# Second feed-forward products by a seven-product scheme on 2x2 blocks, on one Trainium2 core

## The chip, the core and the metric

One core of a Trainium2 chip runs the whole kernel as one program. The metric is the device time of one execution in microseconds; lower is better. A core has TensorE (PE, matmuls; its weight loads are shown apart as PEld), VectorE (DVE), ScalarE (ACT), GpSimd (POOL), SyncE (SP, which here issues DMAs), an on-chip memory SBUF and the accumulator memory PSUM, of which the kernel uses eight banks of 128 x 512 float32.

## The reference

Two blocks of a small transformer trunk over 512 tokens of width 1024, all in float32: a first block with windowed attention, a gated convolution and a mixture of experts, then two layers that each have a mixer and a feed-forward stage. The change touches only these two feed-forward stages:

```python
def sqrelu_mlp(u, w1, w2):
    return jnp.square(jax.nn.relu(u @ w1)) @ w2
...
for layer in range(DEPTH_2):
    ...
    h = h + sqrelu_mlp(rms_norm(h, mlp_norm[layer]), mlp_w1[layer], mlp_w2[layer])
return rms_norm(h, final_norm)
```

`u` is 512 x 1024, `w1` is 1024 x 4096, `w2` is 4096 x 1024.

## The kernel before

**Products.** Every float32 operand is split into a high part (rounded to the type that TensorE takes, `F32R`) and a low part (the rest). A product of two such operands is three matmuls, high by high, high by low and low by high (`mm3`, lines 184 to 188). One matmul has a stationary block of 128 x 128 and a moving block of 128 x 512, and adds into one PSUM bank.

**The feed-forward stage** (`mlp`, from line 1380) goes through the 4096 inner features in four chunks `c` of 1024. In a chunk, the first products (`fm`) make inner slices of 128 features x 512 tokens: four weight units `m{l}u{c}{u}` of 1024 x 256, two slices each, eight slices, 24 matmuls per slice. A slice goes from its bank through `evac`: relu on ScalarE (line 1391), square on VectorE (1392), high part on ScalarE (1393), low part on VectorE (1394), into `hTh` and `hTl`, four tiles of 8 KB per partition in all. Then the second products: for each half `n` of the 1024 output columns and each half `u` of the chunk's features one weight unit `m{l}d{c}{n}/{u}` of 512 x 512. `tm` keeps four banks, one for each 128 tokens, over both units, and `add_x` (line 374, VectorE) adds each full bank to the residual `x`. In the last half of the last chunk `tm_rows` goes row block by row block, so that `step` can normalise one block of 128 tokens (for the next mixer, or for the output) while the next is computed.

**Weights.** `Weights.units` is the list of all weight blocks in the order of use (`plan`, `plan_mlp`). `dma` loads one as raw float32 from SyncE's queue (line 72); `split` makes its high part on ScalarE (line 92) and its low part on VectorE (line 93), in two halves of 128 x 1024 each. `take` gives a unit to the products; `done` gives its two tiles back and calls `ahead`, which splits up to two units ahead (`cuts`) and loads up to four ahead (`look`) as far as there is room.

**Room.** All large tiles lie in 19 slots (`NQ`) of 8 KB per partition: a raw block takes one, a split unit two, `x` two, the split input `xT` of the stage four (`self.xq`, given back at the last chunk). `q` takes the slot that has been free for the longest, and whoever writes it waits until its last user is done. `reserve` (set by `need`) keeps slots back from the weights for tiles that come soon.

**Order.** The kernel is written as one stream of operations; the framework orders each engine's instructions by their dependencies, earlier ones first among those that it takes to be ready, and sets the semaphores. Engines then run their own lists strictly in order.

Of the kernel before, what the change touches and what calls it, by code (L numbers as in the profile page):

```python
# [12 lines left out]
F32 = mybir.dt.float32  # L13
F32R = mybir.dt.float32r
BF = mybir.dt.bfloat16
I32 = mybir.dt.int32
AF = mybir.ActivationFunctionType
OP = mybir.AluOpType
AX = mybir.AxisListType

T = 512
# [27 lines left out]
class Weights:  # L49
# [14 lines left out]
    def add(self, key, shape, parts, whole=False):  # L64
        self.units.append((key, shape, parts, whole))

    def dma(self):
        i = self.n_dma
        key, shape, parts, _ = self.units[i]
        r = self.k.q(shape, F32, "wr")  # L70
        for sl, src in parts:
            self.k.nc.sync.dma_start(r[sl], src)
        self.raw[i] = r
        self.n_dma += 1

    def split(self):
        i = self.n_cut
        if i == self.n_dma:
            self.dma()
        k, nc = self.k, self.k.nc  # L80
        key, shape, parts, whole = self.units[i]
        r = self.raw.pop(i)
        self.n_cut += 1
        if whole:
            self.cut[i] = (r,)
            return
        h = k.q(shape, F32R, "wh")
        lo = k.q(shape, F32R, "wl")
        a, n = shape[-2] // 2, (slice(None),) * (len(shape) - 2)
        for s, eng in zip((slice(0, a), slice(a, shape[-2])), self.engines or (nc.vector, nc.vector)):  # L90
            s = (*n, s)
            nc.scalar.copy(h[s], r[s])  # L92
            eng.tensor_tensor(lo[s], r[s], h[s].bitcast(F32), op=OP.subtract)  # L93
        k.put(r)
        self.cut[i] = (h, lo)

    def ahead(self):
        cut, dma = self.cuts, self.look
        n, r, f = self.limit or len(self.units), self.reserve, self.k.freeq
        def ready():  # L100
            return sum(not u[3] for u in self.units[self.n_take:self.n_cut])
        while self.n_cut < n and ready() < cut and len(f) >= r + 2 + (self.n_cut == self.n_dma):
            self.split()
        r += 2 * max(0, cut - ready())
        while self.n_dma < min(self.n_take + dma, n) and len(f) >= r + 1:
            self.dma()
# [15 lines left out]
class Kern:  # L122
# [67 lines left out]
    def tm(self, key, xT, nk, n, evac, pump=0):  # L190

        for full in self.tm_gen(key, xT, nk, n, evac):
            if full:
                self.pump(pump)
# [477 lines left out]
def kt(w, p=128):  # L672
    return w.rearrange("(k p) f -> p k f", p=p)
# [7 lines left out]
class Trunk(Kern):  # L681
    def plan(self):
# [64 lines left out]
            tm(f"co{n}", I["c_w_out_2"][0], n * 512, 512)  # L747
        self.plan_mlp(1, fm, tm)

    def plan_mlp(self, l, fm, tm):  # L750
        w1, w2 = self.I["mlp_w1_2"][l], self.I["mlp_w2_2"][l]
        for c in range(4):
            for u in range(4):
                fm(f"m{l}u{c}{u}", w1, c * 1024 + u * 256, 256)
            for n in range(2):
                tm(f"m{l}d{c}{n}", w2[c * 1024:(c + 1) * 1024], n * 512, 512)


    def consts(self):
# [619 lines left out]

    def mlp(self, l, xT):  # L1380
        nc, wk = self.nc, self.wk
        for c in range(4):
            hs = [self.q([128, 4, T], F32R, "hTh") for _ in range(2)]
            ls = [self.q([128, 4, T], F32R, "hTl") for _ in range(2)]
            for us in ((0, 1), (2,), (3,)) if c == 0 else ((0,), (1,), (2,), (3,)):
                def evac(f, b):
                    g = us[0] * 2 + f
                    r = wk.tile([128, T], F32, name="relu", tag="a2", bufs=8)
                    s = wk.tile([128, T], F32, name="cv", tag="a2", bufs=8)
                    h, lo = hs[g // 4][:, g % 4], ls[g // 4][:, g % 4]  # L1390
                    nc.scalar.activation(r, b, AF.Relu)
                    nc.vector.tensor_mul(s, r, r)
                    nc.scalar.copy(h, s)
                    nc.vector.tensor_tensor(lo, s, h.bitcast(F32), op=OP.subtract)
                self.fm([f"m{l}u{c}{u}" for u in us], xT, 2, evac)
            if c == 3:
                self.put(*self.xq)
                self.need(4)
            hT = [(hs[k // 4][:, k % 4], ls[k // 4][:, k % 4]) for k in range(8)]
            for n in range(2):  # L1400
                if c < 3 or n == 0:
                    self.tm(f"m{l}d{c}{n}", hT, 4, 512, self.add_x(n))
                    continue
                if l == 0:
                    yT, step = self.norm_T(self.gain(self.I["attn_norm_2"][1]))
                else:
                    yT, step = None, self.final()
                self.tm_rows(f"m{l}d{c}{n}", hT, 512, self.add_x(n), step)
            self.put(*hs, *ls)
        return yT  # L1410

    def topk(self, sc):
# [594 lines left out]
```

## Time and profile before

| | |
|---|---|
| median of 3 runs | 2027.82 us (2024.48 to 2027.97) |
| profiled execution | 2025.49 us |
| its span | 2023.4 us |
| feed-forward stages in the span | about 1000 to 1350 us and 1647 to 2013 us |
| TensorE busy | 1917.4 us (95%) |
| VectorE busy | 1246.3 us (62%) |
| ScalarE busy | 900.1 us (44%) |
| GpSimd busy | 328.4 us (16%) |
| moved by DMA | 260.45 MB, 129 GB/s on average |

The span is the time from the first to the last instruction that the hardware profiler recorded; the execution's time has some 2 us around it. An engine's share is an average over very different stages; what a change in one stage is worth is read from that stage alone.

### The profile page before, as it was taken

What the parts mean: (1) busy time and instruction counts of PE and PEld (TensorE: products, weight loads), DVE (VectorE), ACT (ScalarE), POOL (GpSimd) and SP (SyncE); (2) the same over time, 40 slices, a digit from 0 to 9 for tenths busy, and PEclk for the clock granted to TensorE, in tenths of its full rate; (3) what the DMA queues carried; (4) which work ended last, traced back from release to release, by engine and by line L of the source; (5) the groups of instructions that cost most, each with busy time, mean ns of one, the idle gap of its engine ahead of it and who ended that gap; (6) DMA issues with size and microseconds to landing.
All of it is one profiled execution on the core that took longest, in us unless ns stands there. A gap on an engine that the chain in (4) does not pass through costs nothing.

```text
span 2023.4 us, 25745 instructions
## 1 busy us (share of the span) xinstructions
PE 1917.4 (95%) x9419; PEld 1510.2 (75%) x9419; DVE 1246.3 (62%) x2606; ACT 900.1 (44%) x1697; POOL 328.4 (16%) x436
## 2 busy tenths in 40 slices
PE   7999999699988699999999999999999999999997
PEld 6877887455544587687888888888878888888886
DVE  6865255697667679997544343456789954443343
ACT  4256222586666435547232232422589933232240
POOL 3022000143232001104200000020247620000001
PEclk9999999699999899999999999999999999999999
DMA  7111357699999411104232322342000133323221
GB/s 223 42 43 64 103 191 277 213 354 344 356 368 373 129 42 64 51 32 146 74 122 87 104 94 85 113 136 67 22 22 1 64 120 120 99 88 104 84 84 42
DMA packets 129156, 260.45 MB, mean 129 GB/s; under 512 B 9015, under 2 KB 63631, under 8 KB 129026
## 3 DMA queue, kind: packets, MB, share of 16 engines
q1 hardware_dynamic: 119554, 229.59, 32.4%
q0 software_dynamic: 5952, 16.52, 3.4%
q10 hardware_dynamic: 3520, 12.65, 1.6%
q8 instruction: 76, 1.25, 0.3%
q14 instruction: 54, 0.44, 0.1%
HBM read 245.89 MB, written 14.88 MB: 129 GB/s over the span
## 4 chain that ended last, share of the span: by engine, by line
PE 71%; DVE 11%; DMA 9%; ACT 4%; issue 3%; POOL 1%; SPq 0%; ACTq 0%; DVEq 0%; POOLq 0%
PE ps L188 18%; PE ps L186 18%; PE ps L187 18%; DMA wr<-in_w_up_e_dram 3%; PE ps L580 3%; DVE wl L93 3%; DMA wr<-in_w_gate_e_dram 2%; PE ps L539 2%; PE ps L1249 2%; DMA xd<-y,sidx 1%; ACT wh L92 1%; PE ps L479 1%; PE ps L481 1%; PE ps L292 1%; ACT P L505 1%
## 5 line engine op out<-in xcount | busy, mean ns | idle before, releaser
L93 DVE TENSOR_TENSOR wl<-wr,wh 128x1024 fp32r<-128x1024 f32 (+3 forms) x366 | 439.8, 1224 | 341.4 <-ACT wh L92 322.3
L92 ACT CAST wh<-wr 128x1024 fp32r<-128x1024 f32 (+3 forms) x366 | 368.5, 1036 | 516.2 <-PE ps L188 161.2
L186 PE MATMUL ps<-xTh,wh 128*128 128x512 f32 (+1 forms) x864 | 324.6, 376 | 0.3 <-ACT P L505 0.3
L188 PE MATMUL ps<-xTh,wl 128*128 128x512 f32 (+1 forms) x864 | 323.0, 374 | 0.3 <-DVE wl L93 0.3
L187 PE MATMUL ps<-xTl,wh 128*128 128x512 f32 (+1 forms) x864 | 323.2, 374 | 0.0
L186 PE MATMUL ps<-wh,hTh 128*128 128x512 f32 x512 | 199.4, 389 | 0.0
L188 PE MATMUL ps<-wh,hTl 128*128 128x512 f32 x512 | 199.2, 389 | 0.0
L187 PE MATMUL ps<-wl,hTh 128*128 128x512 f32 x512 | 199.2, 389 | 0.0
L188 PEld LDWEIGHTS ps<-xTh,wl 128*128 128x128 f32 x864 | 162.7, 188 | 29.3 <-DVE wl L93 0.8
L186 PEld LDWEIGHTS ps<-xTh,wh 128*128 128x128 f32 x864 | 162.8, 188 | 28.9 <-ACT P L505 0.6
L187 PEld LDWEIGHTS ps<-xTl,wh 128*128 128x128 f32 x864 | 162.9, 189 | 28.2 <-issue 0.2
L300 POOL TENSOR_TENSOR xn<-x,gB 128x1024 f32<-128x1024 f32 x16 | 38.4, 2401 | 734.4 <-DVE x L374 734.4
L374 DVE TENSOR_TENSOR x<-ps,x 128x512 f32<-128x512 f32 x88 | 60.7, 690 | 127.1 <-PE ps L188 127.1
L505 ACT ACTIVATE P<-ps,sm 128x512 f32<-128x512 f32 (+1 forms) x224 | 118.3, 532 | 16.1 <-DVE sm L493 12.9
L1200 PE MATMUL ps<-wl,xgT 128*112 128x512 f32 x256 | 111.2, 434 | 13.9 <-DVE wl L93 13.4
L186 PE MATMUL ps<-wh,xTh 128*128 128x512 f32 (+3 forms) x320 | 120.5, 377 | 0.9 <-DVE ik L435 0.9
L1249 PE MATMUL ps<-wr,hT 128*72 128x512 f32 x256 | 117.4, 594 | 4.0 <-ACT hT L1238 4.0
L188 PE MATMUL ps<-wh,xTl 128*128 128x512 f32 (+3 forms) x320 | 117.5, 368 | 0.7 <-DVE xTl L352 0.7
L187 PE MATMUL ps<-wl,xTh 128*128 128x512 f32 (+3 forms) x320 | 117.0, 367 | 0.0
L1199 PE MATMUL ps<-wh,xgT 128*112 128x512 f32 x256 | 109.5, 428 | 3.0 <-ACT wh L92 2.8
L187 PEld LDWEIGHTS ps<-wl,hTh 128*128 128x128 f32 x512 | 96.1, 188 | 20.0
L188 PEld LDWEIGHTS ps<-wh,hTl 128*128 128x128 f32 x512 | 96.1, 188 | 19.9
(452 smaller groups left out, 3510.9 us busy)
## 6 DMA issues: line engine op xcount, KB each, us to landing
wr<-in_mlp_w_dram SPq DMA_DIRECT2D x64, 1024.0 KB
wr<-in_w_gate_e_dram SPq DMA_DIRECT2D x64, 512.0 KB
wr<-in_w_up_e_dram SPq DMA_DIRECT2D x64, 512.0 KB
wr<-in_w_down_e_dram SPq DMA_DIRECT2D x32, 1024.0 KB
wr<-in_w_in_dram SPq DMA_DIRECT2D x17, 1024.0 KB
wr<-in_ab_w_in_dram SPq DMA_DIRECT2D x10, 1024.0 KB
wr<-in_c_w_in_dram SPq DMA_DIRECT2D x6, 1024.0 KB
wr<-in_w_out_dram SPq DMA_DIRECT2D x4, 1024.0 KB
```

The source lines that it names most:

```text
L92: nc.scalar.copy(h[s], r[s])
L93: eng.tensor_tensor(lo[s], r[s], h[s].bitcast(F32), op=OP.subtract)
L186: mm(ps, ah, bh, start=first, stop=False)
L187: mm(ps, ah, bl, start=False, stop=False)
L188: mm(ps, al, bh, start=False, stop=last)
L374: self.nc.vector.tensor_tensor(xs, b, xs, op=OP.add)
L505: nc.scalar.activation(P[s][:, p:p + c.stop - c.start], b[:, c], AF.Exp, bias=m[:, 0, t:t + 1], accum_out=m[:, 1, t:t + 1])
L539: nc.tensor.transpose(b[:, c:c + 128], P[s][:, p:p + 128], self.idf)
L580: nc.tensor.matmul(o, v, x[:, cs], start=start, stop=a.closes and g == 2 and z == len(vx) - 1, skip_group_check=True)
L1199: nc.tensor.matmul(b[0:M], x, h, start=first, stop=False)
L1200: nc.tensor.matmul(b[0:M], x, lo, start=False, stop=last)
L1249: nc.tensor.matmul(b[0:HM], hq[:, k], w[0][:, k, s], start=k == 0, stop=k == 1)
```

## The change

The chunk's second product, tokens x features by features x columns, is seen as a product of 2 x 2 blocks: the 512 tokens are two halves of 256, the chunk's 1024 features are the even and the odd slices, the 1024 output columns are two halves of 512. Instead of the eight block products it makes seven (Strassen's method in its form with shared sums), of sums of weight blocks and sums of activation blocks, both made in float32 on VectorE before the split into high and low parts:

- **Weight blocks.** `add7` puts seven units per chunk on the list in place of four. Four of them load a block (b11, b12, b22, b21, of 512 x 512, every other group of 128 features); four units form a difference in place first (`sums`), and raw blocks stay until the last unit that needs them (`free`). A unit that loads nothing is passed over by `dma`.
- **Activations.** `evac` works on pairs of slices. Of the even one it splits the first 256 tokens (`A11`, in work tiles) and forms one difference of 256 columns; of the odd one it splits all (`B2`), forms one sum of 256, splits it with the difference (`S31`), forms two more differences of 256, and splits these (`S24`). Six tiles of 8 KB hold what four held.
- **Products.** Each of the seven is 2 x 12 matmuls (two blocks of 128 tokens, 4 slices, 3 matmuls) of the same shapes as before. Products share banks: after each product `add_x` adds the bank as it stands to one quarter of `x`, and a later product adds on in the same bank (`home`). The order is 11, T1, T2, 22, T3, 21, T4, in the last chunk 11, T1, T2, 22, 21, T3, T4, there with `step` for the first two row blocks after 21 and for the last two after their parts of T4. In the first layer's last chunk the four slots of the next stage's input are taken before the second products, not in their middle.

```diff
--- before.py
+++ after.py
@@ -64,12 +64,30 @@
     def add(self, key, shape, parts, whole=False):
         self.units.append((key, shape, parts, whole))
 
+    def add7(self, key, shape, parts, order):
+
+        b11, b12, b21, b22 = parts
+        rec = {"11": (b11, 0, [], 0, ()), "T1": (b12, 1, [(0, 1, 0)], 0, ()), "T2": (b22, 2, [(0, 2, 0)], 0, ()),
+               "22": (None, 0, [(1, 2, 1)], 2, (2,)), "T3": (None, 0, [], 1, (1,)),
+               "21": (b21, 3, [(0, 3, 0)], 3, (3,)), "T4": (None, 0, [], 0, (0,))}
+        group = {}
+        for o in order:
+            load, place, sums, src, free = rec[o]
+            self.units.append((f"{key}/{o}", shape, load, (group, place, sums, src, free)))
+
     def dma(self):
         i = self.n_dma
-        key, shape, parts, _ = self.units[i]
+        key, shape, parts, how = self.units[i]
+        if parts is None:
+            self.n_dma += 1
+            return
         r = self.k.q(shape, F32, "wr")
         for sl, src in parts:
             self.k.nc.sync.dma_start(r[sl], src)
+        if isinstance(how, tuple):
+            how[0][how[1]] = r
         self.raw[i] = r
         self.n_dma += 1
 
@@ -79,26 +97,33 @@
             self.dma()
         k, nc = self.k, self.k.nc
         key, shape, parts, whole = self.units[i]
-        r = self.raw.pop(i)
+        r = self.raw.pop(i, None)
         self.n_cut += 1
-        if whole:
+        if whole is True:
             self.cut[i] = (r,)
             return
+        sums, frees = (), (r,)
+        if whole:
+            g, _, sums, src, frees = whole
+            sums = [[g[x] for x in y] for y in sums]
+            r, frees = g[src], [g[x] for x in frees]
         h = k.q(shape, F32R, "wh")
         lo = k.q(shape, F32R, "wl")
         a, n = shape[-2] // 2, (slice(None),) * (len(shape) - 2)
         for s, eng in zip((slice(0, a), slice(a, shape[-2])), self.engines or (nc.vector, nc.vector)):
             s = (*n, s)
+            for d, x, y in sums:
+                nc.vector.tensor_tensor(d[s], x[s], y[s], op=OP.subtract)
             nc.scalar.copy(h[s], r[s])
             eng.tensor_tensor(lo[s], r[s], h[s].bitcast(F32), op=OP.subtract)
-        k.put(r)
+        k.put(*frees)
         self.cut[i] = (h, lo)
 
     def ahead(self):
         cut, dma = self.cuts, self.look
         n, r, f = self.limit or len(self.units), self.reserve, self.k.freeq
         def ready():
-            return sum(not u[3] for u in self.units[self.n_take:self.n_cut])
+            return sum(u[3] is not True for u in self.units[self.n_take:self.n_cut])
         while self.n_cut < n and ready() < cut and len(f) >= r + 2 + (self.n_cut == self.n_dma):
             self.split()
         r += 2 * max(0, cut - ready())
@@ -747,13 +772,21 @@
             tm(f"co{n}", I["c_w_out_2"][0], n * 512, 512)
         self.plan_mlp(1, fm, tm)
 
+    order = "11", "T1", "T2", "22", "T3", "21", "T4"
+    late = "11", "T1", "T2", "22", "21", "T3", "T4"
+
     def plan_mlp(self, l, fm, tm):
+        W = self.W
         w1, w2 = self.I["mlp_w1_2"][l], self.I["mlp_w2_2"][l]
         for c in range(4):
             for u in range(4):
                 fm(f"m{l}u{c}{u}", w1, c * 1024 + u * 256, 256)
-            for n in range(2):
-                tm(f"m{l}d{c}{n}", w2[c * 1024:(c + 1) * 1024], n * 512, 512)
+
+            v = kt(w2[c * 1024:(c + 1) * 1024])
+            a = (slice(None),) * 3
+            W.add7(f"m{l}d{c}", [128, 4, 512],
+                   [[(a, v[:, i::2, n * 512:(n + 1) * 512])] for i in range(2) for n in range(2)],
+                   self.late if c == 3 else self.order)
 
 
     def consts(self):
@@ -1379,34 +1412,100 @@
 
     def mlp(self, l, xT):
         nc, wk = self.nc, self.wk
+        sub, add = OP.subtract, OP.add
+        H = T // 2
         for c in range(4):
-            hs = [self.q([128, 4, T], F32R, "hTh") for _ in range(2)]
-            ls = [self.q([128, 4, T], F32R, "hTl") for _ in range(2)]
+
+            B2, S31, S24 = [[self.q([128, 4, T], F32R, f"hT{i}") for i in "hl"] for _ in range(3)]
+            A11 = [wk.tile([128, 4, H], F32R, name="a11", tag="a4", bufs=3) for _ in "hl"]
+            z = {}
+
+            def split(dst, k, x):
+                nc.scalar.copy(dst[0][:, k], x)
+                nc.vector.tensor_tensor(dst[1][:, k], x, dst[0][:, k].bitcast(F32), op=sub)
+
+            def evac(g, b):
+                k = g // 2
+                r = wk.tile([128, T], F32, name="relu", tag="a2", bufs=8)
+                s = z[g % 2] = wk.tile([128, T], F32, name="cv", tag="a2", bufs=8)
+                nc.scalar.activation(r, b, AF.Relu)
+                nc.vector.tensor_mul(s, r, r)
+                tt = nc.vector.tensor_tensor
+                if g % 2 == 0:
+                    split(A11, k, s[:, 0:H])
+                    z["y"] = y = wk.tile([128, T], F32, name="cv", tag="a2", bufs=8)
+                    tt(y[:, 0:H], s[:, 0:H], s[:, H:T], op=sub)
+                    return
+                split(B2, k, s)
+                y, e = z["y"], z[0]
+                tt(y[:, H:T], e[:, H:T], s[:, H:T], op=add)
+                split(S31, k, y)
+                w = wk.tile([128, T], F32, name="cv", tag="a2", bufs=8)
+                tt(w[:, 0:H], y[:, H:T], e[:, 0:H], op=sub)
+                tt(w[:, H:T], s[:, 0:H], w[:, 0:H], op=sub)
+                split(S24, k, w)
+
             for us in ((0, 1), (2,), (3,)) if c == 0 else ((0,), (1,), (2,), (3,)):
-                def evac(f, b):
-                    g = us[0] * 2 + f
-                    r = wk.tile([128, T], F32, name="relu", tag="a2", bufs=8)
-                    s = wk.tile([128, T], F32, name="cv", tag="a2", bufs=8)
-                    h, lo = hs[g // 4][:, g % 4], ls[g // 4][:, g % 4]
-                    nc.scalar.activation(r, b, AF.Relu)
-                    nc.vector.tensor_mul(s, r, r)
-                    nc.scalar.copy(h, s)
-                    nc.vector.tensor_tensor(lo, s, h.bitcast(F32), op=OP.subtract)
-                self.fm([f"m{l}u{c}{u}" for u in us], xT, 2, evac)
+                self.fm([f"m{l}u{c}{u}" for u in us], xT, 2, lambda f, b: evac(us[0] * 2 + f, b))
+            yT, step = None, None
             if c == 3:
                 self.put(*self.xq)
-                self.need(4)
-            hT = [(hs[k // 4][:, k % 4], ls[k // 4][:, k % 4]) for k in range(8)]
-            for n in range(2):
-                if c < 3 or n == 0:
-                    self.tm(f"m{l}d{c}{n}", hT, 4, 512, self.add_x(n))
-                    continue
                 if l == 0:
+                    self.need(4)
                     yT, step = self.norm_T(self.gain(self.I["attn_norm_2"][1]))
                 else:
-                    yT, step = None, self.final()
-                self.tm_rows(f"m{l}d{c}{n}", hT, 512, self.add_x(n), step)
-            self.put(*hs, *ls)
+                    step = self.final()
+            lo, hi = slice(0, H), slice(H, T)
+            left = {"11": (A11, lo), "T1": (S31, hi), "T2": (S24, lo), "22": (S24, hi), "T3": (S31, lo),
+                    "21": (B2, lo), "T4": (B2, hi)}
+
+            home = {"11": ("u", 0, 0), "T1": ("v", 1, 1), "T2": ("u", 0, 1), "22": ("v", 0, 1), "T3": ("u", 1, 1),
+                    "21": ("w", 0, 0), "T4": ("u", 1, 0)}
+            banks = {}
+            order = self.late if c == 3 else self.order
+
+            def product(o, i, hl):
+
+                at, th, n = home[o]
+                new = (at, i) not in banks
+                if new:
+                    banks[at, i] = self.bank()
+                b, (a, cols) = banks[at, i], left[o]
+                s = slice(cols.start + i * 128, cols.start + (i + 1) * 128)
+                for k in range(4):
+                    mm = nc.tensor.matmul
+                    mm(b, a[0][:, k, s], hl[0][:, k], start=new and k == 0, stop=False, skip_group_check=True)
+                    mm(b, a[0][:, k, s], hl[1][:, k], start=False, stop=False, skip_group_check=True)
+                    mm(b, a[1][:, k, s], hl[0][:, k], start=False, stop=k == 3, skip_group_check=True)
+                self.add_x(n)(th * 2 + i, b)
+                if o in ("22", "21", "T4"):
+                    self.free(banks.pop((at, i)))
+
+            for o in order[:5]:
+                hl = self.W.take(f"m{l}d{c}/{o}")
+                for i in range(2):
+                    product(o, i, hl)
+                    if o == order[4] and step and i:
+                        step(0)
+                self.W.done(hl)
+            if step:
+
+                step(1)
+                us = [self.W.take(f"m{l}d{c}/{o}") for o in order[5:]]
+                for i in range(2):
+                    product(order[5], i, us[0])
+                for i in range(2):
+                    product(order[6], i, us[1])
+                    step(2 + i)
+                for hl in us:
+                    self.W.done(hl)
+            else:
+                for o in order[5:]:
+                    hl = self.W.take(f"m{l}d{c}/{o}")
+                    for i in range(2):
+                        product(o, i, hl)
+                    self.W.done(hl)
+            self.put(*B2, *S31, *S24)
         return yT
 
     def topk(self, sc):
```

## Rows read from the trace of the kernel before

**Rows 1.** Busy time of each engine, its share of the span and its instructions: the page.

```profile
span 2023.4 us, 25745 instructions
...
PE 1917.4 (95%) x9419; PEld 1510.2 (75%) x9419; DVE 1246.3 (62%) x2606; ACT 900.1 (44%) x1697; POOL 328.4 (16%) x436
```

**Rows 2.** Stretches: us; busy us (count) of PE, PEld, DVE, ACT, POOL; granted clock; DMA share, GB/s.

```profile
1020.00:1330.00 310.00, 310.00 (x1377) 257.00 (x1377) 125.70 (x146) 94.36 (x119) 0.00 (x0) 1.00 0.29 96
1680.00:2012.00 332.00, 332.00 (x1492) 276.04 (x1492) 137.75 (x181) 95.57 (x125) 7.18 (x3) 1.00 0.27 89
```

**Rows 3.** Chain of waits in the first stage, 1000 to 1330 us, shares by line.

```profile
by line: PE ps L188 32.5%; PE ps L186 32.5%; PE ps L187 32.4%; DVE wl L93 1.0%; PE ps L348 0.3%; ACT wh L92 0.3%; DVE xn L301 0.2%; DVE nst L319 0.2%; DVE xTl L352 0.2%; issue 0.1%; DVE nst L323 0.1%; DVE nst L315 0.1%; DVE nst L316 0.0%; D
```

**Rows 4.** One of the three matmul lines of the second products: count, shortest/median/longest ns.

```profile
L186 PE MATMUL ps<-wh,hTh x512: 389/389/481, 1043.6 to 2012.3; 128*128 128x512 f32 x171
```

**Rows 5.** Timeline of VectorE, two of one unit's four adds to x: start, us.

```profile
1147.21 0.69 DVE L374 TENSOR_TENSOR x<-ps,x 128x512 f32<-128x512 f32 x1 [1.35 <-PE ps L188]
1149.93 0.69 DVE L374 TENSOR_TENSOR x<-ps,x 128x512 f32<-128x512 f32 x1 [2.03 <-PE ps L188]
```

**Rows 6.** Timeline of VectorE, four instructions with no idle time between them.

```profile
1099.15 1.23 DVE L93 TENSOR_TENSOR wl<-wr,wh 128x1024 fp32r<-128x1024 f32 x1 [3.64 <-ACT wh L92]
1100.29 0.69 DVE L1392 TENSOR_TENSOR cv<-relu 128x512 f32<-128x512 f32 x1
1100.89 1.22 DVE L93 TENSOR_TENSOR wl<-wr,wh 128x1024 fp32r<-128x1024 f32 x1
1102.03 0.68 DVE L1394 TENSOR_TENSOR hTl<-cv,hTh 128x512 fp32r<-128x512 f32 x1
```

**Rows 7.** Groups by form, 1007 to 1327 us: busy us, mean ns | idle before, releasers.

```profile
L93 DVE TENSOR_TENSOR wl<-wr,wh 128x1024 fp32r<-128x1024 f32 x58 | 69.8, 1221 | 99.8 <-ACT wh L92 97.0 <-PE ps L188 2.7
L92 ACT CAST wh<-wr 128x1024 fp32r<-128x1024 f32 x59 | 60.5, 1049 | 161.0 <-PE ps L187 68.3 <-PE ps L188 63.7 <-issue 26.6
...
L374 DVE TENSOR_TENSOR x<-ps,x 128x512 f32<-128x512 f32 x28 | 19.3, 690 | 46.4 <-PE ps L188 46.4
```

**Rows 8.** Groups by form, VectorE, whole span: other shapes.

```profile
L1044 DVE TENSOR_TENSOR h<-x,gB 128x1024 f32<-128x1024 f32 x4 | 8.0, 1999 | 0.1
...
L400 DVE TENSOR_TENSOR hsq<-cs 128x256 f32<-128x256 f32 x4 | 1.7, 415 | 0.0
```

**Rows 9.** Busy time by stretch, expert stage and attention; columns as in rows 2.

```profile
540.00:550.00 10.00, 8.14 (x25) 3.73 (x25) 6.44 (x11) 4.90 (x11) 4.19 (x7) 1.00 1.03 316
...
790.00:800.00 10.00, 8.52 (x47) 5.93 (x46) 9.86 (x24) 7.02 (x21) 2.93 (x5) 1.00 0.23 76
800.00:802.00 2.00, 1.89 (x6) 1.05 (x6) 1.94 (x5) 1.01 (x3) 0.59 (x1) 0.67 0.47 155
802.00:804.00 2.00, 2.00 (x5) 0.86 (x5) 1.58 (x6) 1.45 (x3) 0.86 (x3) 0.50 0.00 0
...
810.00:820.00 10.00, 10.00 (x50) 7.51 (x49) 9.71 (x21) 4.54 (x9) 1.37 (x3) 1.00 0.00 1
820.00:830.00 10.00, 10.00 (x46) 8.29 (x45) 9.62 (x24) 1.78 (x3) 0.00 (x0) 1.00 0.20 59
```

**Rows 10.** Timeline of ScalarE behind the end of a first-product unit.

```profile
1098.06 1.05 ACT L92 CAST wh<-wr 128x1024 fp32r<-128x1024 f32 x1 [3.28 <-PE ps L187]
1099.02 0.59 ACT L1391 ACTIVATE relu<-ps 128x512 f32<-128x512 f32 x1
```

**Rows 11.** DMA from 1098 to 1118 us, forty slices of 0.5 us; SyncE's issues.

```profile
GB/s 0 0 0 0 0 0 0 0 0 0 49 106 356 401 414 410 352 8 0 0 0 0 0 0 0 0 0 0 0 0 0 0 82 115 430 393 406 406 266 0
...
1102.14 22.09 SPq L72 DMA_DIRECT2D wr<-in_mlp_w_dram  x3
```

**Rows 12.** Timeline of VectorE at the end: the last two row blocks.

```profile
2007.71 0.69 DVE L374 TENSOR_TENSOR x<-ps,x 128x512 f32<-128x512 f32 x1 [0.30 <-PE ps L188]
...
2013.15 0.69 DVE L374 TENSOR_TENSOR x<-ps,x 128x512 f32<-128x512 f32 x1 [0.31 <-PE ps L188]
...
2017.46 0.75 DVE L301 TENSOR_SCALAR xn<-xn,nst 128x1024 f32<-128x1024 f32 x1
```

## The prediction

> **What bounds the kernel now.** I read the busy times first. TensorE is busy for 1917.4 of 2023.4 us, VectorE for 62% of it and ScalarE for 44% [rows 1]. Then the two feed-forward stages by themselves: in 310 us of the first and 332 us of the second TensorE is never idle and its granted clock is 1.00 (the upper level, 2.4 GHz), while VectorE is busy for 125.7 us (41%) and 137.8 us (41%) [rows 2]. Third, the chain of waits in the first of these stages: 97% of it is the three matmul lines [rows 3]. So here a matmul taken away is time taken away, until another engine makes TensorE wait. Outside these stages the change touches nothing.
>
> **Matmuls removed.** The second products have three lines of 512, 1536 matmuls, now [rows 4]. One shows 389 ns, but they overlap: a bank of 12 matmuls is added to x every 2.72 us [rows 5], so one costs 2.72/12 = 0.227 us. A chunk (1024 inner features) has 8 block products of 24 matmuls before and 7 after; one product is 5.44 us. Eight chunks (4 in each of 2 layers) save 8 x 5.44 = 43.5 us. The shapes stay 128x128 by 512. Adding into a bank that has been evacuated already is not shown before; a first matmul of a bank and a later one have the same 389 ns [rows 4], so I price it as they are, at both ends.
>
> **Work added to VectorE, per chunk.** Its instructions overlap a little: with 1024 columns the next starts 1.14 us later, with 512 columns 0.60 us [rows 6], although they show 1.22 and 0.69 us [rows 7]; for 256 columns I take 0.34 us from 415 ns [rows 8] in the same way.
> Weight splits: 7 units in place of 4, 2 subtractions each: +6 x 1.14 = 6.8 us.
> Sums of weight blocks: 4 units, 2 each: 8 x 1.14 = 9.1 us. A plain float32 one of 1024 columns is hardly there before: the split's subtraction (1.22 us) has the same operands but for the output's type, another is 2.00 us [rows 8]. I take the first, since with 512 columns the two output types show 0.69 and 0.68 us [rows 6]; the second is the upper bound, the lower is that nothing changes.
> Adds to x: 14 in place of 8: +6 x 0.60 = 3.6 us.
> Activations: per pair of inner slices 6 instructions of 512 and 3 of 256 columns, then 2 more of 256 in front: 5 x 0.60 + 5 x 0.34 = 4.7 us against 4 x 0.60; four pairs: +9.2 us.
> Together +28.7 us on some 33 us, so 62 us in a chunk of 81.6 us: 76%. ScalarE gets 6 more copies of 1.05 us and a few small ones [rows 7] and stays below half. In bulk it all lies beside TensorE. That VectorE can be run this full is shown elsewhere in the same kernel: between 810 and 830 us it is busy 97% and TensorE 100% [rows 9].
>
> **Where it does not fit.** 19 slots of 8 KB carry everything: x takes 2, the split input 4, inner activations 6 in place of 4. That leaves 7 in place of 9: two for the product in use, two for the next, three for raw blocks that the sums still need. So a product's split can't start until the product two before it has given back its slots, as splits already wait for TensorE (68.3 + 63.7 = 132 us of ScalarE's waits in this stage) [rows 7], only now for 5.44 us products instead of 10.9 us units. Let t=0 be the end of the chunk's last first-product matmul. "T1" can be split only from then (it takes the slots of the last first-product unit), and so can the last inner slice. ScalarE first does T1's copy, then the relu, as now [rows 10], so VectorE starts at 1.1 us. Up to the first half of T2 it has T1's 2 subtractions (2.28), the last slice (4 x 0.60 + 3 x 0.34 = 3.4), two adds (1.2), T2's two sums (2.28, in place over what T1's split reads, so not earlier) and one subtraction (1.14): 10.3 us, done at 11.4; T2 is due at 10.9: 0.5 us of wait. From there to the first half of "22": T2's other subtraction, three adds, two sums, one subtraction, 1.14 + 1.8 + 2.28 + 1.14 = 6.4 us in 5.44: 0.9 us, with some 0.1 for semaphores. I take 1.5 us a chunk: 12 us. After "22" it is light (T3 and T4 have no sums, 21's fit in beside T3's split, and the next chunk's first-product units run at 10.9 us each), and the last first-product slices are due only at the fourth matmul group of T1.
>
> **Loads.** Bytes are the same, one DMA of 1 MB per block. Only in the first layer's last chunk, where 21 is put ahead of T3 and the slots of the old input go straight to the next stage's, block 21's load has to wait for T2's slot. A load issued at 1102.1 is through at 1106.5 us: 4.4 us [rows 11]. Then sum, copy and subtraction, 1.14 + 1.05 + 1.22 = 3.4 us; 7.8 against 5.44: 2.4 us, once. The second layer has four slots more and loads it earlier: nothing there.
>
> **Tail.** The last two row blocks now end 2.72 us apart instead of 5.44, and from add to normalised row is 5.1 us (2013.15 to 2018.21) [rows 12]; so the last row's add can sit behind its forerunner's small VectorE steps: between 0 and 2.5 us; I take 1.5 us for each layer, 3 us.
>
> **Sum.** -43.5 + 12 + 2.4 + 3 = -26.1 us. Against the profiled execution's own 2025.5 us (span 2023.4) this is 1999.4; that execution lies 2.3 us under the runs' median of 2027.8, on which the forecast stands: 2027.8 - 26.1 = 2002 us.
>
> **A rule against it.** TensorE's clock stays at 1.00 through stretches of the expert stage where TensorE is busy for only 81% in short pieces (540 to 550 us), but around 800 us it falls to 0.50 (the lower level, 1.2 GHz) after ten us of attention at 85% busy [rows 9]. The Trainium skill, "TensorE: Matmul & The Clock Gate", section "A second HAM failure mode: psum-queue depth-cycling", says that short idle times between groups of matmuls that cycle through banks can make the clock swing. The change makes such groups; by the rule each chunk would lose a fall, by the rows of the expert stage none. I follow the rows, as a wait of 1 us in 38 leaves TensorE at 97%.
>
> **Rivals.**
> (a) VectorE keeps up, no waits: 43.5 us saved, less 0 to 3 for the tail, 1984 to 1987. For it: the schedule already fills VectorE's waits (split, square, split, subtraction start 1.14, 0.60, 1.14 us apart) [rows 6], and some sums may run before t=0. Against: 10.3 us of work by 10.9.
> (b) VectorE's order becomes the bound, slower. Each split with sums is sum, copy on ScalarE, subtraction, for two halves; if nothing fills VectorE's wait for the copy, one costs 2 x (1.14 + 1.05 + 1.14) + 1.2 of adds = 7.9 against 5.44 us, at T2, 22 and 21: 7.4 us a chunk, 2 more than is saved; 8 x 2 + 5.4 = 21 us slower, 2049. It decides once a chunk waits longer than 5.44 us less the ends' share, about 4.8 us. For it: few slots, so no split is ready two products ahead. Against: the filled order [rows 6], the 97% [rows 9].
> (c) Waits of 3 to 4.8 us a chunk, because the sums cost the upper bound of 2.00 us (4 x 0.78 = 3.1 us more ahead of T2 and 22): 4.6 x 8 = 37 in place of 12: 2027, no change to speak of.
> (d) The clock swings. A fall as around 800 us (2 us at 0.67 and 2 us at 0.50) costs 0.67 + 1.0 = 1.7 us [rows 9]; one in each chunk 13 us: 2015.
>
> **Chances.** The forecast, with 0.4 to 3 us of wait a chunk (1993 to 2014): 0.60. (a) 0.17. (d) 0.03. (c) 0.08, half of it still faster by over 0.2%. (b) 0.12. 0.2% is 4 us, about what runs of this kernel can tell apart. Faster: 0.60 + 0.17 + 0.03 + 0.04 = 0.84; same 0.04; slower 0.12. The range goes from (a) without a tail, 1984, to the upper bound of the sums, 2026; only (b) and the worst of (c) lie outside.
>
> **What would show it.** Right: 1344 matmuls in the second products, still 2.72 us per 12; TensorE's idle time between 1000 and 2010 us about 15 to 18 us more, put down to VectorE's weight splits at the second and fourth products; VectorE near 75% in the stages. Wrong: long waits at T3, T4 or the first products (slots, not VectorE, would be short); a clock below 1.00; more than 2.4 us of waiting for a load; VectorE's instructions longer than the rows say; or no waits at all.

## The result and the profile after

The changed kernel takes 1992.5 us (median of 4 runs, 1990.2 to 1993.7) against 2026.2 us: ratio 0.9837, interval 0.9825 to 0.985, faster by 33.7 us. Forecast were 2002 us (from 2027.8 us, the median of the three runs known then) and a gain of 26.1 us.

The page of the changed kernel, busy times and two of its strips of forty slices:

```profile
span 1988.5 us, 25850 instructions
...
PE 1877.9 (94%) x9219; PEld 1475.6 (74%) x9227; DVE 1475.0 (74%) x2958; ACT 977.2 (49%) x1809; POOL 336.8 (17%) x436
...
DVE  6865154697767679998677868785789956786868
...
PEclk9999999799999899999999999999999999999999
```

Against [rows 1] TensorE is busy 39.5 us less and VectorE 229 us more, which is the forecast 28.7 us in each of eight chunks (230 us). One chunk by stretch, and one of the three matmul lines of the products (with the tiles `hTh` and, apart, with the work tiles `a`; the other two lines have the same counts):

```profile
1082.00:1164.00 82.00, 82.00 (x362) 67.54 (x362) 63.27 (x84) 35.15 (x46) 0.00 (x0) 1.00 0.31 103
```

```profile
L1477 PE MATMUL ps<-wh,hTh x384: 388/389/501, 1043.7 to 1976.2; 128*128 128x512 f32 x192
...
L1477 PE MATMUL ps<-wh,a x64: 389/389/389, 1038.2 to 1941.8; 128*128 128x512 f32 x64
```

Three lines of 384 + 64 are the 1344 matmuls that were forecast, at the same 389 ns as in [rows 4]; VectorE is busy 63.3 of 82 us (77%; forecast 76%; [rows 2] had 41%).

Where the time went is read from marks in the timelines: the start of the relu of a chunk's first slice, and of the last add to `x`. From mark to mark, in us:

| | before | changed |
|---|---|---|
| first layer, chunks 1, 2, 3 | 79.39, 87.04, 87.04 | 74.18, 81.92, 81.90 |
| first layer, last chunk to its last add | 83.74 | 83.21 |
| from there to the second layer's first relu | 327.46 | 331.80 |
| second layer, chunks 1, 2, 3 | 79.38, 87.04, 87.04 | 74.25, 81.90, 81.92 |
| second layer, last chunk to its last add | 81.60 | 78.33 |
| all | 999.7 | 969.4 |

Six chunks save 30.9 of the possible 6 x 5.44 = 32.6 us. The first layer's last chunk, with the stage behind it, is 3.8 us slower though 5.44 us of matmuls are gone; the second layer's saves 3.3. In all 30.3 us. Of the rest of this profile's difference (spans of 2023.4 and 1988.5 us), 5.4 us lie ahead of the first mark (1013.4 and 1008.1 us), and 0.8 us are lost behind the last add.

Most of the 5.4 us is a difference between executions: over the runs below the mark moves between 1008 and 1014 us. But 1.8 us belong to the change. From one and the same instruction some 70 us ahead, the mark comes after 74.06 us in the kernel before, and after 72.24 to 72.31 us in the changed kernel and in every variant below. In the kernel before, a weight split of VectorE runs there beside GpSimd's product with the norm's gain, in front of the last row block's norm:

```profile
995.62 2.42 POOL L300 TENSOR_TENSOR xn<-x,gB 128x1024 f32<-128x1024 f32 x1 [3.92 <-DVE x L374]
995.97 3.15 DVE L93 TENSOR_TENSOR wl<-wr,wh 128x1024 fp32r<-128x1024 f32 x1 [0.43 <-ACT wh L92]
```

It takes 3.15 us in place of 1.22. In the changed kernel no split stands there; that six tiles leave two slots less than four did would explain it, but this was not tested.

Just ahead of a burst and in it, timelines of VectorE in the changed kernel, last chunk of the first layer (L116 sums of weight blocks, L118 splits' subtractions; product 11 starts at 1283.9 us):

```profile
1276.85 1.22 DVE L116 TENSOR_TENSOR wr<-wr 128x1024 f32<-128x1024 f32 x1
1278.92 1.22 DVE L116 TENSOR_TENSOR wr<-wr 128x1024 f32<-128x1024 f32 x1
1280.99 1.22 DVE L116 TENSOR_TENSOR wr<-wr 128x1024 f32<-128x1024 f32 x1
1283.40 1.22 DVE L116 TENSOR_TENSOR wr<-wr 128x1024 f32<-128x1024 f32 x1
...
1291.29 1.21 DVE L116 TENSOR_TENSOR wr<-wr 128x1024 f32<-128x1024 f32 x1
...
1293.03 1.22 DVE L116 TENSOR_TENSOR wr<-wr 128x1024 f32<-128x1024 f32 x1
1294.16 1.22 DVE L118 TENSOR_TENSOR wl<-wr,wh 128x1024 fp32r<-128x1024 f32 x1
...
1297.63 1.21 DVE L118 TENSOR_TENSOR wl<-wr,wh 128x1024 fp32r<-128x1024 f32 x1
```

Four sums, those of T1 and of 22, start before product 11 does; only T2's two lie in the burst. T2's first subtraction ends at 1295.38 us; TensorE, on its timeline, comes for it a little earlier:

```profile
1294.59 0.39 PE L1479 MATMUL ps<-wh,hTl 128*128 128x512 f32 x1
1294.82 0.61 PE L1477 MATMUL ps<-wh,hTh 128*128 128x512 f32 x2
1295.43 0.50 PE L1478 MATMUL ps<-wl,hTh 128*128 128x512 f32 x1
```

This is T2's start, on time at 1294.82 and then some 0.3 us behind: the whole wait of a chunk (the other chunks show the same). The subtraction for 22 (1297.63) is through 1.8 us before TensorE wants it.

The first layer's tail, by TensorE's waits, by stretch, by VectorE's splits and by GpSimd's products with the gain (timelines):

```profile
1307.09 0.73 PE L1477 MATMUL ps<-wh,hTh 128*128 128x512 f32 x2 [0.91 <-ACT wh L117]
1308.35 0.51 PE L1478 MATMUL ps<-wl,hTh 128*128 128x512 f32 x1 [0.53 <-DVE wl L118]
...
1333.30 0.50 PE L211 MATMUL ps<-wh,xTh 128*128 128x512 f32 x1 [2.81 <-DVE xTl L377]
```

```profile
1305.00:1315.00 10.00, 8.57 (x37) 6.46 (x36) 8.52 (x9) 4.87 (x5) 3.14 (x5) 1.00 0.73 224
1320.00:1325.00 5.00, 2.48 (x13) 1.49 (x12) 5.00 (x18) 2.94 (x3) 0.52 (x1) 1.00 0.00 0
1330.00:1335.00 5.00, 2.19 (x10) 1.62 (x9) 5.00 (x6) 2.12 (x4) 5.00 (x3) 0.87 1.00 365
1335.00:1340.00 5.00, 5.00 (x22) 4.05 (x21) 4.09 (x19) 0.02 (x1) 1.59 (x2) 0.79 0.71 222
```

```profile
1312.87 1.22 DVE L118 TENSOR_TENSOR wl<-wr,wh 128x1024 fp32r<-128x1024 f32 x1
1315.21 3.07 DVE L118 TENSOR_TENSOR wl<-wr,wh 128x1024 fp32r<-128x1024 f32 x1
...
1318.92 2.68 DVE L118 TENSOR_TENSOR wl<-wr,wh 128x1024 fp32r<-128x1024 f32 x1
...
1329.87 2.78 DVE L118 TENSOR_TENSOR wl<-wr,wh 128x1024 fp32r<-128x1024 f32 x1
...
1333.89 2.07 DVE L118 TENSOR_TENSOR wl<-wr,wh 128x1024 fp32r<-128x1024 f32 x1
```

```profile
1314.77 2.42 POOL L325 TENSOR_TENSOR xn<-x,gB 128x1024 f32<-128x1024 f32 x1 [5.83 <-DVE x L399]
1317.14 3.38 POOL L325 TENSOR_TENSOR xn<-x,gB 128x1024 f32<-128x1024 f32 x1
1328.77 2.79 POOL L325 TENSOR_TENSOR xn<-x,gB 128x1024 f32<-128x1024 f32 x1 [8.24 <-DVE x L399]
1331.53 3.35 POOL L325 TENSOR_TENSOR xn<-x,gB 128x1024 f32<-128x1024 f32 x1
```

TensorE is idle for 1.4, 2.5 and 2.8 us in the first three of these stretches, and its granted clock is 0.87 and 0.79 in the last two (1.7 us less work, by 5 x 0.13 + 5 x 0.21). The splits that take 2.1 to 3.1 us in place of 1.22 are those that begin while GpSimd runs, and each of the four ends 1.08 or 1.09 us after a GpSimd instruction has ended (1318.28 after 1317.19, 1321.60 after 1320.52, 1332.65 after 1331.56, 1335.96 after 1334.88). So the split gets nowhere until GpSimd is through, and the next GpSimd instruction, which begins while the split still runs, takes 3.35 or 3.38 us in place of 2.40. Even a norm step of one column waits like this (second layer's tail; such a step takes 0.16 us elsewhere):

```profile
1978.23 2.34 POOL L325 TENSOR_TENSOR xn<-x,gB 128x1024 f32<-128x1024 f32 x1 [0.89 <-DVE x L399]
1978.31 2.27 DVE L348 SCALAR_TENSOR_TENSOR nst<-nst 128x1 f32<-128x1 f32 x1
```

In the feed-forward tails of the kernel before no split ran beside that instruction; where the mixers pass into the feed-forward stages two did, the one at 995.97 us above and one at 1663.29 us of 2.29 us.

### The profile page after: what moved, and what is told of

Its sections match the earlier page's. It is cut to its first block, busy times and chain, and to the rows that moved or that the text cites. A ratio compares the mean times of both kernels' runs of the same rounds, so it can differ in the third digit from the quotient of the medians.

```text
span 1988.5 us, 25850 instructions
## 1 busy us (share of the span) xinstructions
PE 1877.9 (94%) x9219; PEld 1475.6 (74%) x9227; DVE 1475.0 (74%) x2958; ACT 977.2 (49%) x1809; POOL 336.8 (17%) x436
## 4 chain that ended last, share of the span: by engine, by line
PE 70%; DVE 12%; DMA 10%; ACT 4%; issue 3%; POOL 1%; SPq 0%; ACTq 0%; DVEq 0%; POOLq 0%
PE ps L211 13%; PE ps L213 13%; PE ps L212 13%; PE ps L1478 5%; PE ps L1477 5%; PE ps L1479 5%; DMA wr<-in_w_up_e_dram 4%; DVE wl L118 3%; PE ps L605 3%; PE ps L564 2%; DMA wr<-in_w_gate_e_dram 2%; DMA xd<-y,sidx 1%; PE ps L317 1%; ACT wh L117 1%; PE ps L1282 1%
## 5 line engine op out<-in xcount | busy, mean ns | idle before, releaser
L118 DVE TENSOR_TENSOR wl<-wr,wh 128x1024 fp32r<-128x1024 f32 x414 | 502.1, 1233 | 194.6 <-ACT wh L117 129.4
L117 ACT CAST wh<-wr 128x1024 fp32r<-128x1024 f32 x414 | 415.9, 1037 | 349.7 <-DVE wl L118 61.5
L213 PEld LDWEIGHTS ps<-xTh,wl 128*128 128x128 f32 x864 | 163.1, 189 | 28.7
L1478 PE MATMUL ps<-wl,hTh 128*128 128x512 f32 x384 | 150.6, 392 | 1.3 <-DVE wl L118 1.3
L1477 PE MATMUL ps<-wh,hTh 128*128 128x512 f32 x384 | 148.3, 390 | 2.2 <-DVE nst L348 1.3
L1479 PE MATMUL ps<-wh,hTl 128*128 128x512 f32 x384 | 149.5, 389 | 0.0
L399 DVE TENSOR_TENSOR x<-ps,x 128x512 f32<-128x512 f32 x136 | 92.9, 686 | 52.2 <-PE ps L213 26.8
L325 POOL TENSOR_TENSOR xn<-x,gB 128x1024 f32<-128x1024 f32 x16 | 42.5, 2661 | 388.9 <-DVE x L399 388.9
L548 POOL TENSOR_SCALAR P<-P,sm,gt 128x512 f32<-128x512 f32 (+3 forms) x128 | 82.2, 653 | 116.2 <-DVE sm L543 104.7
L564 PE MATMUL ps<-idf,P 128*128 128x128 f32 x560 | 93.7, 276 | 5.0 <-POOL P L548 3.9
```

The costliest lines, as they stand in the source:

```text
L213: mm(ps, al, bh, start=False, stop=last)
L564: nc.tensor.transpose(b[:, c:c + 128], P[s][:, p:p + 128], self.idf)
L1477: mm(b, a[0][:, k, s], hl[0][:, k], start=new and k == 0, stop=False, skip_group_check=True)
L1478: mm(b, a[0][:, k, s], hl[1][:, k], start=False, stop=False, skip_group_check=True)
L1479: mm(b, a[1][:, k, s], hl[0][:, k], start=False, stop=k == 3, skip_group_check=True)
```

## The experiments

Two questions: why do the chunks hardly wait, and what is lost in the tail? All ratios are to the kernel before.

**Sums held back (e3).** Two instructions of one column make each sum wait for the slots of its split.

```diff
             for d, x, y in sums:
+                e = (*s, slice(0, 1))
+                nc.vector.tensor_copy(h[e], y[e])
+                nc.vector.scalar_tensor_tensor(y[e], h[e].bitcast(F32), 0.0, y[e], op0=OP.mult, op1=OP.add)
                 nc.vector.tensor_tensor(d[s], x[s], y[s], op=OP.subtract)
```

> The changed kernel with each sum of weight blocks made to wait for the slots of its split, by two VectorE instructions of one column per slice ahead of it, so that no sum can run ahead. Theory (the chunks hardly wait because the sums of T1 and 22 run in VectorE's idle time beside the first products, ahead of the burst): the burst that the prediction summed comes back, TensorE waits 1 to 2 us a chunk at T2 and 22 for weight splits, 8 to 16 us slower in all, 2000 to 2008. Rival (the burst was only priced too high and has room with the sums in it): waits stay under 0.3 us a chunk, within 2 us of 1992.5.

Measured: 2025.3 us, ratio 1.000 (0.999 to 1.0009). All of the gain is gone. VectorE and TensorE in this run, second layer (product 11 starts at 1797.6 us, so T2 is due at 1808.5; L119 sums, L121 subtractions):

```profile
1798.01 1.23 DVE L119 TENSOR_TENSOR wr<-wr 128x1024 f32<-128x1024 f32 x1
...
1799.76 1.22 DVE L119 TENSOR_TENSOR wr<-wr 128x1024 f32<-128x1024 f32 x1
...
1808.10 2.36 DVE L119 TENSOR_TENSOR wr<-wr 128x1024 f32<-128x1024 f32 x2
...
1810.98 2.35 DVE L121 TENSOR_TENSOR wl<-wr,wh 128x1024 fp32r<-128x1024 f32 x2
```

```profile
1810.51 0.73 PE L1480 MATMUL ps<-wh,hTh 128*128 128x512 f32 x2 [1.64 <-ACT wh L120]
...
1812.25 0.50 PE L1481 MATMUL ps<-wl,hTh 128*128 128x512 f32 x1 [1.01 <-DVE wl L121]
```

T1's sums now lie behind the start of product 11, T2's begin at 1808.1, and TensorE waits 1.64 + 1.01 us. A chunk takes 85.0 us in the second layer and 86.6 to 87.9 in the first, against 81.9. The slowest of them by stretch:

```profile
1090.00:1178.00 88.00, 85.36 (x362) 69.54 (x361) 65.38 (x100) 35.40 (x47) 0.00 (x0) 0.96 0.30 96
```

VectorE's share is 74%, less than the changed kernel's 77%, and yet the chunk is 5.9 us longer: what counts is when the work is due. The theory holds in kind; its size was too small, since T1's sums are in the burst as well, and since in the first layer's chunks the granted clock falls behind these waits (0.96 here, 1.00 in the second layer). Part of the loss is the edit's own (two short instructions per half, some 0.2 us), so the run bounds what running ahead is worth rather than measures it.

**Sums left out (e5).**

```diff
-            for d, x, y in sums:
+            for d, x, y in []:
```

> The changed kernel with the sums of weight blocks left out (64 VectorE instructions of 1.22 us; the products then use the raw blocks). Theory (the sums lie beside TensorE except block 21's in the first layer's last chunk): 1 to 3 us faster, 1989.5 to 1991.5, chunks still 81.9 us. Rival (VectorE's load still reaches the path in each chunk): 0.3 us a chunk and more in the tails, 6 us or more faster, under 1986.5.

Measured: 1995.0 us, ratio 0.9846 (0.9831 to 0.9861): nothing won. Chunks take 81.60 us, that is 15 x 5.44, so the 0.3 us are what the sums cost there; both theories missed, as neither foresaw the tail, which was slower without them (84.5 us for the last chunk, 333.8 for the stage behind). There TensorE waits 3.7 us at a stretch for the next stage's first operand, against 2.8, and from 1330 to 1345 us its clock is 0.83, 0.50 and 0.65 in steps of 5 us, against 0.87, 0.79 and 1.00. Why fewer instructions lead to longer waits there was not followed.

**Subtractions doubled (e4).**

```diff
-            eng.tensor_tensor(lo[s], r[s], h[s].bitcast(F32), op=OP.subtract)
+            for _ in range(2 if whole else 1):
+                eng.tensor_tensor(lo[s], r[s], h[s].bitcast(F32), op=OP.subtract)
```

> The changed kernel with the subtraction of each split of the seven units written twice (the second writes the same values): 14 more VectorE instructions of 1.14 us a chunk, 63 + 16 = 79 of 82 us. Theory (it is the burst between the last first product and product 22 that counts, not VectorE's share): 3.4 us more work before T2 is due and 3.4 us more before 22, against 0.2 and 2.3 us of room: waits of 3 to 6 us a chunk, 24 to 48 us slower, 2016 to 2040. Rival (only the share counts, 97% still fits): under 1 us a chunk, 1993 to 2000.

Measured: 2112.4 us, ratio 1.043 (1.041 to 1.0449). A chunk takes 95.7 us, 13.8 more, over twice the theory's upper end; the rival (share alone) is out. TensorE's idle time is 8.0 us of it. The excess has a second part. Three stretches inside one chunk of this run:

```profile
1240.00:1245.00 5.00, 4.52 (x19) 3.04 (x17) 5.00 (x8) 0.76 (x2) 0.00 (x0) 1.00 0.00 0
1245.00:1250.00 5.00, 0.96 (x3) 0.48 (x3) 4.91 (x6) 3.76 (x4) 0.00 (x0) 0.87 0.00 0
1250.00:1255.00 5.00, 4.55 (x11) 3.60 (x12) 3.26 (x4) 0.00 (x0) 0.00 (x0) 0.50 0.00 0
```

TensorE is idle for 4.0 of 5 us, and in the next 5 us its granted clock is 0.50 (1.2 GHz): with 4.55 us busy, some 2.3 us more lost there. So once waits are long enough, the clock adds its own. Rival (d) of the prediction is real, but not at the 0.3 us that a chunk of the changed kernel waits.

**GpSimd out of the tails (e1).** The gain is multiplied on VectorE, in one instruction with the scaling.

```diff
-                    yT, step = self.norm_T(self.gain(self.I["attn_norm_2"][1]))
+                    yT, step = self.norm_T(self.gain(self.I["attn_norm_2"][1]), False)
...
-            self.norm_rows(self.xr(t), gB, y, True)
+            self.norm_rows(self.xr(t), gB, y, False)
```

> The changed kernel (1992.5 us) with the multiplication by the gain at the two feed-forward tails on VectorE in one instruction with the scaling, instead of on GpSimd. Theory (GpSimd and VectorE hinder each other in the tail): no split's subtraction over 1.3 us there (before: 3.07, 2.68, 2.78, 2.07 us), TensorE's idle time between 1303 and 1335 us falls from 7.5 us to about 3 us, and the whole is 4 to 6 us faster, 1987 to 1988. Rival (the tail is slow because its row blocks end 2.72 us apart and VectorE has the norms of two at once): VectorE gets 0.5 us more per row block, so 0 to 3 us slower, 1992 to 1996.

Measured: 1988.4 us, ratio 0.9814 (0.9801 to 0.9828). VectorE's groups in the first layer's tail of this run:

```profile
L118 DVE TENSOR_TENSOR wl<-wr,wh 128x1024 fp32r<-128x1024 f32 x10 | 12.1, 1220 | 0.6 <-ACT wh L117 0.6
```

The same ten splits took 17.8 us (mean 1792 ns) in the changed kernel. With GpSimd gone they are at 1220 ns: the hindrance is shown. The loads are not its cause, as the DMA engines are as busy as before in the same stretch (share 1.02 in the first line below, against 1.00 above). In each layer's last chunk about 2 us come back (81.1 and 76.4 us). But TensorE's idle time in the first layer's tail falls only from 7.5 to 5.8 us, not to the theory's 3, and the clock falls lower than in the changed kernel:

```profile
1330.00:1335.00 5.00, 1.99 (x10) 1.66 (x11) 5.00 (x13) 2.12 (x4) 1.16 (x1) 0.82 1.02 334
1335.00:1340.00 5.00, 5.00 (x13) 3.84 (x13) 3.93 (x14) 0.00 (x0) 0.56 (x1) 0.50 0.99 320
```

**Slots later (e2).**

```diff
                 if l == 0:
-                    self.need(4)
-                    yT, step = self.norm_T(self.gain(self.I["attn_norm_2"][1]))
+                    gB = self.gain(self.I["attn_norm_2"][1])
...
                 hl = self.W.take(f"m{l}d{c}/{o}")
+                if o == order[4] and c == 3 and l == 0:
+                    yT, step = self.norm_T(gB)
```

> The changed kernel with the four slots of the next stage's input taken before block product 21 of the first layer's last chunk instead of before product 11. Theory (block 21's load waits there for a slot): no wait of VectorE or TensorE for that load, TensorE's 1.4 us at about 1307 us gone, 1 to 2 us faster, 1990.5 to 1991.5. Rival (that wait only stands in front of the next one, the slow split of T4): no change, within 0.5 us.

Measured: 1989.3 us, ratio 0.9821 (0.9807 to 0.9834). The wait for block 21 (0.91 + 0.53 us at 1307 us) is gone, and the stage behind takes 327.1 us again in place of 331.8; more than the wait itself. A part of the difference is the clock, which is 1.00 throughout this run's tail.

**Both (e6).**

> The changed kernel with both tail edits: gain on VectorE, and the next stage's four slots taken before block product 21. Theory (two separate losses in the first layer's tail, GpSimd against VectorE and the wait for block 21's load): the gains add, 1985 to 1987. Rival (both only uncover the chain of the last row blocks' norms): as the better one alone, 1988 to 1989.5.

Measured: 1982.0 us, ratio 0.9783 (0.9768 to 0.9797), beyond the theory and the fastest version of the study. The tail's 50 us in this run:

```profile
1306.00:1356.00 50.00, 49.65 (x234) 40.01 (x233) 40.03 (x91) 19.20 (x28) 4.95 (x8) 1.00 0.52 179
```

TensorE is idle for 0.35 us and its clock is 1.00. Each edit alone leaves a wait of 2.6 us for the next stage's first operand (`xTl`); with both it is 0.3 us (e1, e2 and this run):

```profile
1334.11 0.79 PE L211 MATMUL ps<-wh,xTh 128*128 128x512 f32 x1 [2.56 <-DVE xTl L377]
...
1332.32 0.50 PE L211 MATMUL ps<-wh,xTh 128*128 128x512 f32 x1 [2.65 <-DVE xTl L377]
...
1330.36 0.50 PE L211 MATMUL ps<-wh,xTh 128*128 128x512 f32 x1 [0.33 <-DVE xTl L377]
```

That wait, and the clock that falls in e1, are why the gains more than add. With both edits the kernel saves 42.6 us between the marks, of 43.5.

**The first layer's last chunk undone (e7, e10, with e9 beside it).** Four units, eight products, row by row, as in the kernel before.

```diff
+            if l == 0 and c == 3:
+                for n in range(2):
+                    tm(f"m{l}d{c}{n}", w2[c * 1024:(c + 1) * 1024], n * 512, 512)
+                continue
...
+            if l == 0 and c == 3:
+                yT = self.mlp_last(l, c, xT)
+                continue
```

> The changed kernel with the last chunk of the first layer undone: four weight units, eight block products, the last half row block by row block. 5.44 us of matmuls come back. Theory (the seven-product order in this chunk costs more at the tail than the 5.44 us that it saves): the last chunk takes 83.7 us and the stage after it 327.5 us as in the kernel before, 3 to 5 us faster than the changed kernel, 1987.5 to 1989.5. Rival (the loss lies in what the next stage finds in the slots): the stage after stays near 332 us, 0 to 1 us slower, 1992.5 to 1993.5.

Measured: 1993.6 us, ratio 0.9839 (0.9826 to 0.9852), so no gain in the whole, though chunk and stage behind were as the theory said (83.8 and 326.9 us) and the marks 965.2 us apart against 969.4. Single times went from 1988.9 to 1994.6. So it was set beside the changed kernel itself:

> The changed kernel itself, on one chip beside the next run, since undoing the first layer's last chunk gave 965.2 us from the first relu of the stages to the last add against 969.4, but whole times that did not differ. Theory (stages before the feed-forward stages move the whole by 2 to 3 us between executions): 992 to 994 us behind 1000, that is 1992 to 1994, with the same 969 to 970 us in the stages.

> The first layer's last chunk undone, again, on the same chip as the run before. Theory (the seven-product order costs more than it saves there): 965 to 966 us in the stages, and 2.5 to 5 us faster than the run before in the whole. Rival (what the stages gain is lost elsewhere): equal in the whole within 1.5 us.

Measured: 1992.4 us (0.9837, 0.9824 to 0.9851) and 1988.3 us (0.9817, 0.9803 to 0.983); between the marks 970.3 and 965.2 us. (In e9, the changed kernel again, the clock falls to 0.67 and 0.64 in two stretches of the first layer's tail; in e7 and e10 it stays at 1.00 there.) Here the 5 us show in the whole, 4.1 us. Taken with e7, undoing is worth 0 to 4 us: by the marks the seven-product order costs more in this one chunk than it saves, while the whole time of e7 doesn't confirm it.

**Undone, and the final norm on VectorE (e8).**

> The edit of the run before and, in the final norm alone, the gain on VectorE. Theory (GpSimd hinders VectorE in the last tail too, 2 us as the last chunk of the second layer showed with that edit: 76.4 us for 78.3): 2 us less than the run before, 1985.5 to 1987.5. Rival (with only the final norm edited nothing is left to win): equal to the run before within 0.5 us.

Measured: 1989.0 us, ratio 0.9816 (0.9801 to 0.9831); the second layer's last chunk takes 76.35 us for 78.36, the forecast 2 us, and the whole is 4.6 us under e7. It stays behind e6, which keeps the seven products everywhere.

## Why the prediction was right, and where it was not

**Bound and matmuls: right.** 1344 matmuls, 2.72 us per 12, 43.5 us taken away on TensorE's path. Wrong is "Outside these stages the change touches nothing": 1.8 us are won ahead of the first mark.

**VectorE's load: right.** 63.3 us of 82 against 62 of 81.6. (For a pair of slices the words count six instructions of 512 columns; the sum takes five, and so has the code.)

**The burst: right in place, one term too many.** The prediction put 1.5 us of wait in each chunk, at T2 and 22. Measured: 0.3 us in a full chunk, all of it at T2, where 0.5 was forecast; T2's first subtraction ends 11.45 us after the last first product (1283.93 to 1295.38), where 11.4 was summed. The step that failed is "From there to the first half of 22: T2's other subtraction, three adds, two sums, one subtraction": 22's two sums are not there, they run beside the first products, before t=0. They write raw blocks in place, need no slot, and the order lets them go ahead; the prediction said so of "some sums" in its rival (a) and left them in the sum all the same. Without their 2.28 us, 22's 6.4 become 4.1 us in 5.44: no wait. e3 shows how much hangs on it. The term was 12 us; it measured 1.8 us (32.6 less 30.9, six chunks, the last ones being counted with the tails).

**Block 21's load: right in kind.** 2.4 us forecast, 0.91 + 0.53 us measured, and in the place that was named. e2 removes it, and wins 4.1 us in the first layer's last chunk and the stage behind: taking the slots early cost more than this wait.

**The tails: too small.** 3 us forecast for both layers. By the marks the first layer loses 3.8 + 5.44 = 9.2 us there, 1.4 of it block 21, and the second 5.44 - 3.3 = 2.2 us. The step that failed is "so the last row's add can sit behind its forerunner's small VectorE steps": the prediction asked only whether these steps queue, not what they and the splits cost while GpSimd forms two rows' products with the gain, nor what TensorE's waits then do to its clock. In the kernel before, the adds of the first layer's row blocks came 5.1 to 6.7 us apart and no split was due then; now two row blocks come together, with the splits of T4 and of the next stage. The row of 3.15 us at 995.97 us stood in the trace of the kernel before and could have been read.

In the second layer this is nearly all: with GpSimd out (e1) 2.0 of the 2.2 us come back. In the first layer e1 gives back 1.9 of the 9.2 us, the later slots (e2) 4.1, and both together 10.3. So there the loss is the two edits' causes together, with the clock's part in it, and not GpSimd alone.

**Sum.** -43.5 + 1.8 + 9.2 + 2.2 = -30.3 us between the marks, against -26.1: the burst was 10 us too dear and the tails with the load 6 us too cheap. The two errors partly cancelled, so the total was nearer than its parts: that is luck. With 1.8 us ahead of the marks and 0.8 us lost behind them it is 31.3 of the 33.7 us; the other 2.4 us lie between executions, as far as can be told.

**Rivals.** (a) is nearly what the chunks do; the time lies between (a), up to 1987, and the forecast's own 1993. (b) did not happen, but e3 and e4 show its two ways in: without the sums ahead the gain is gone, and with 14 more instructions a chunk it is a loss of 86 us. (c) is out: a sum takes 1.22 us, the row taken, not 2.00. (d) does not occur in the chunks (clock 1.00); it shows in the first layer's tail, in e3's chunks of the first layer and, fully, in e4. The Trainium skill's rule that was weighed ("TensorE: Matmul & The Clock Gate", "A second HAM failure mode: psum-queue depth-cycling") therefore doesn't decide here: cycling through banks with 0.3 us of wait in 82 left the clock up; idle time of 4 us brought it down.

**Its signs of being wrong.** Two came, both in the first layer's tail: VectorE's instructions longer than the rows say, and a clock below 1.00. And TensorE's idle time between the marks grew by 7.7 us (9.9 to 17.6), not by 15 to 18, with its longest waits at the norms and at the next stage's first operand, not at T2 and 22.

## What to carry to other kernels

Saving matmuls by extra elementwise work paid here, where TensorE is the bound, but what must be priced is the burst between two due times, not the share of the busy engine; and in that burst first ask which operations need nothing that the burst frees, since they will have run before. Work that is spread over several engines in a tail needs a second look as soon as something is moved closer together. When two small losses stand one behind the other, remove both before judging either.

## What the runs showed of the hardware

A VectorE instruction with two operands in SBUF took 2.07 to 3.07 us beside a GpSimd instruction that reads two operands there, in place of 1.22 us, and ended 1.08 or 1.09 us after that one's end; one of a single column took 2.27 us in place of 0.16. The GpSimd ones that began while a split ran took 3.35 and 3.38 us in place of 2.40. The Trainium skill states this contention in "SBUF — State Buffer", section "Who interferes with whom": a VectorE instruction with two SBUF inputs contends with a GpSimd instruction that reads SBUF. The trace agrees, and e1, where the GpSimd instruction is gone and the same splits are at 1220 ns, shows the cause.

TensorE's granted clock was 1.00 in the chunks of the changed kernel but for the first layer's tail, where it was 0.87 and 0.79 behind a wait of 2.8 us. It was 0.50 in the 5 us that followed 4.0 us of idle time (e4).
